# Two-block transformer kernel: order of the second attention, gate rows through memory, a stacked identity

## The chip, the cores and the metric

One NeuronCore of one Trainium2 chip runs the whole kernel. The metric is device microseconds of one execution; before the change the median of three runs is 2517.28 us (2514.53 to 2517.49).

## The reference, cut to what matters

Two transformer blocks on one sequence of 256 tokens, width 2048, all in float32. The first block has a gated convolution, a forgetting attention, a gate merge and a squared-ReLU feed-forward. The second block, which most of the change touches, is:

```python
mod = silu(c) @ w_ada + b_ada                      # six rows of 2048
shift_m, scale_m, gate_m, shift_f, scale_f, gate_f = split(mod, 6)
h = rms_norm(x, norm_mix_g) * (1 + scale_m) + shift_m
q, k, v, xs, z, bmat, cmat, dt_raw = split(h @ w_in, ...)
attn = rms_norm(attention(q, k, v, rel_bias), attn_norm_g)    # 8 heads of 128
ssm = ssd_mixer(xs, z, bmat, cmat, dt_raw, ...)    # y * silu(z), rms-normed in 2 groups
x = x + gate_m * (concat(attn, ssm) @ w_out)
h = rms_norm(x, norm_ffn_g) * (1 + scale_f) + shift_f
x = x + gate_f * conv_ffn(h, w_up, ..., w_down)
return rms_norm(x, final_norm_g)
```

## The kernel before, in words

**Weights.** Every weight matrix streams through the core once, in pieces of 1 MB. SyncE issues the load (`load`, L62) into one of three buffers `wraw`; ScalarE copies the piece to a rounded half `wH` (L126) and VectorE subtracts to get the rest `wL` (L127), three buffers each. TensorE multiplies both halves with activations that are split in the same way (chunks `act`, four buffers of four 128-channel tiles). `bblock` gives output channels by partition (two halves of 64 matmuls, each in a PSUM tile from a pool of two, evicted by L188 on ScalarE and L190 on VectorE); `ablock` gives tokens by partition (24 matmuls a piece). Nearly all matmuls have the line of the helper `mm`, L133.

**Order.** The body writes straight-line code; a planner orders each engine's instructions by program order as priority and by a simulated time, so that ready work of later stages fills gaps, and it hands out the buffers of a tag as they come free. `tc.high_priority()` lifts what is in it. Each engine then runs its list in order.

**Small sums.** `small_proj` multiplies by a matrix of n = 8 or 16 columns: high and low rows are stacked on 2n partitions, and four matmuls per token tile, with two slices of the identity, add and transpose them (tiles `wft`, `wdtt`; L133). Each such matmul shows as two instructions on TensorE.

**First norm.** After the first projection (`wide`, tiles `cc`) the sum of squares of x is reduced on TensorE (`rs0p`), raised to -1/2 on GpSimd (L290) and spread over the partitions (`bcast_tok`, `rbc0p`). VectorE scales `ccs` by it (L491, L502, L503) beside the projection `cb`.

**Second attention.** The projections q and k of both head groups come first (j = 0: q, k; j = 1: q, k), each with a piece of the state-space mixer in its middle (`ssm_prep`, `ssm_decay`, `ssm_out`). Then for each j: v (`ablock`), four heads (`heads`: scores `s`, softmax, transposes `pt`, product `o`) beside the projection z, then `cat` times silu(z) (L903, L905). `rms_ch` sums squares over `cat` for a norm: `ratt` for the eight heads, `rss0` and `rss1` for the two mixer groups. `cat_split` scales the four chunks of `cat` (L873) and splits them (L317, L318) into `act` buffers, which the four chunks of `h3` hold until the last projection of h3 has read them. The output projection `wo` (`ablock`, four pieces a column block) reads the four chunks in turn.

**Gates.** `mod` holds the six rows with channel as partition. `bcast_cols` turns gate_m (columns 32 to 47, `gm_bc`) and gate_f (80 to 95, `gf2`) into rows on all partitions by 16 transposes each (L306) and 4 copies on ScalarE (L307). `gm_bc` is used after each `wo` block, `gf2` in the down projection. Both lie in the tag `r8` (two buffers), where `gf2` follows the bias tile `toep`.

**End.** The last output block is cut into two halves of 256 columns in one PSUM bank (`dnl`).

Of the kernel before, what the change touches and what calls it, by code (L numbers as in the profile page):

```python
# [7 lines left out]
F32 = mybir.dt.float32  # L8
# [26 lines left out]
@with_exitstack  # L35
def body(ctx: ExitStack, tc: tile.TileContext, x_d, xT_d, vec_d, con_d, rel_d, relc_d, gfin_d, c_d, fg_d,
         wf_d, wdt_d, win_d, wv_d, wco_d, wao_d, wmix_d, wff1_d, wff2_d, wada_d, win2_d, wv2_d, wout_d, wup_d,
         wdn_d, rscr, xscr, out):
    nc = tc.nc
    V, A, T, G = nc.vector, nc.scalar, nc.tensor, nc.gpsimd  # L40

# [7 lines left out]
    def bank(name):  # L49
        return smp.tile([P, 512], F32, tag="sm", name=name)  # L50
# [39 lines left out]
    V.memset(mhalf, -0.5)  # L90
    warm = cp.tile([P, 2], F32, name="warm")
    A.activation(warm, mhalf, AF.Square)

    n_ada = [0]
    n_pc = [0]
# [171 lines left out]
    def small_proj(w_d, n, acts, name):  # L267
        raw = tp.tile([P, KT, n], F32, tag="t1k", bufs=6, name=name + "r")
        load(raw, w_d)
        hl = tp.tile([P, KT, 2, n], FR, tag="t2k", bufs=4, name=name + "hl")  # L270
        split(hl[:, :, 0, :], hl[:, :, 1, :], raw)
        ps = bank(name + "c")
        for k in range(KT):
            mm(ps[0:2 * n, :], hl[:, k].rearrange("p a n -> p (a n)"), acts[k][2], k == 0, k == KT - 1)
        c = tp.tile([P, 2, S], F32, tag="t2k", bufs=4, name=name + "s")
        A.activation(c[0:2 * n].rearrange("p a s -> p (a s)"), ps[0:2 * n, :], AF.Copy)
        tr = bank(name + "t")
        for t in range(2):
            ts = slice(t * P, (t + 1) * P)
            o = tr[:, t * n:(t + 1) * n]  # L280
            mm(o, c[0:2 * n, 1, ts], ident[0:2 * n, n:2 * n], t == 0, False)
            mm(o, c[0:2 * n, 1, ts], ident[0:2 * n, 0:n], False, False)
            mm(o, c[0:2 * n, 0, ts], ident[0:2 * n, n:2 * n], False, False)
            mm(o, c[0:2 * n, 0, ts], ident[0:2 * n, 0:n], False, True)
        return tr

    def pow_rstd(dst, ms_src, inv_n):
# [9 lines left out]
        A.activation(bc, ps[:, :S], AF.Copy)  # L297
        return bc

    def bcast_cols(cols, name):  # L300
        o = r8(name)
        for b in range(4):
            ps = bank(f"{name}p{b}")
            for k in range(4):
                i = 4 * b + k
                T.transpose(ps[:, k * P:(k + 1) * P], cols[:, i:i + 1].to_broadcast([P, P]), ident)  # L306
            A.activation(o[:, b * 512:(b + 1) * 512], ps, AF.Copy)  # L307
        return o

    def two(bc):  # L310
# [163 lines left out]
    with tc.high_priority():  # L474
        sacc = junk().rearrange("p (a s) -> p a s", a=2)
        for i in range(8):
            if i == 0:
                behind(A.activation(sacc, xT[:, 0:2, :], AF.Square), h1_last[0])
            else:
                sq = tp.tile([P, 2, S], F32, tag="t2k", bufs=4, name="sq0")  # L480
                behind(A.activation(sq, xT[:, 2 * i:2 * i + 2, :], AF.Square), h1_last[0])
                V.tensor_tensor(sacc, sacc, sq, op=OP.add)
    ps = bank("rs0p")
    for t in range(2):
        for b in range(2):
            mm(ps[:, t:t + 1], sacc[:, b, t * P:(t + 1) * P], ones[:, 0:1], t == 0 and b == 0, b == 1)
    rs0 = cp.tile([P, 2], F32, name="rs0")
    pow_rstd(rs0, ps[:, 0:2], 1.0 / D)
    rbc = bcast_tok(rs0, "rbc0")
    rbc2 = tp.tile([P, S], F32, tag="rbc2", bufs=1, name="rbc2")  # L490
    V.tensor_tensor(rbc2, rbc, rbc, op=OP.mult)  # L491

    cyh, cyl = cyc[:, :, 0, :], cyc[:, :, 1, :]
    for j in range(2):
# [202 lines left out]
    for c in range(N_FF // 2):  # L697
        if c == N_FF // 2 - 1:
            while n_ada[0] < 96:
                ada()  # L700
            V.tensor_tensor(mod, mod, vec[:, VEC["b_ada"]:VEC["b_ada"] + 96], op=OP.add)
            am = cp.tile([P, 16], F32, name="am")
            V.scalar_tensor_tensor(am, mod[:, 16:32], 1.0, vec[:, VEC["norm_mix_g"]:VEC["norm_mix_g"] + 16],
                                   op0=OP.add, op1=OP.mult)
            af = cp.tile([P, 16], F32, name="af")
            V.scalar_tensor_tensor(af, mod[:, 64:80], 1.0, vec[:, VEC["norm_ffn_g"]:VEC["norm_ffn_g"] + 16],
                                   op0=OP.add, op1=OP.mult)
            fls = rel_tiles()
            toep = r8("toep", (P, 8, S))
            for b in range(2):  # L710
                for k in range(2):
                    tps = bank(f"tps{b}{k}")
                    mm(tps, flip, fls[b][:, 2 * k:2 * k + 2, :].rearrange("p h c -> p (h c)"), True, True)
                    A.activation(toep[:, 4 * b + 2 * k:4 * b + 2 * k + 2, :].rearrange("p h c -> p (h c)"),  # L714
                                 tps, AF.Copy)
        u = us.pop(2 * c) + us.pop(2 * c + 1)
        ff2(c, u, 4 if c < N_FF // 2 - 1 else 3)
        for j in (2 * c + 3, 2 * c + 4):
            if j < N_FF:
                us[j] = ff1(j)  # L720
# [160 lines left out]
    ssm_x(1)  # L881


    qk = []
    for j in range(2):
        for hq, (nb, nm, sc) in enumerate(((0 + j, f"q2{j}", SCALE), (2 + j, f"k2{j}", None))):
            la = ssm_prep(j, hq)
            ms = []
            qk.append(bblock(win2_d, nb, h3, nm, q4([P, 4, S], nm + "T"), scale=sc,
                             mid=lambda: ms.extend(ssm_decay(j, hq, *la))))  # L890
            ssm_out(j, hq, ms, last_mm[0])
    gm_bc = None
    rss = []
    for j in range(2):
        ps = ablock(wv2_d, j, range(4), h3, f"v2{j}")
        vt = q4([P, 2, 512], f"vt2{j}")
        for t in range(2):
            A.activation(vt[:, t, :], ps[t], AF.Copy)
        heads(j, qk[2 * j], qk[2 * j + 1], vt, toep, lambda h, o: V.tensor_copy(cat[:, h, :], o))
        if j:  # L900
            ratt = rms_ch(0, 8, 1.0 / 1024, "ratt")
        z = bblock(win2_d, 6 + j, h3, f"z{j}", q4([P, 4, S], f"zs{j}"),
                   lambda hf, o: A.activation(o, o, AF.Silu))  # L903
        sl = slice(8 + 4 * j, 12 + 4 * j)
        V.tensor_tensor(cat[:, sl, :], cat[:, sl, :], z, op=OP.mult)  # L905
        if j == 0:
            rss.append(rms_ch(8, 4, 1.0 / 512, "rss0"))
            gm_bc = bcast_cols(mod[:, 32:48], "gm_bc")
    gf2 = bcast_cols(mod[:, 80:96], "gf2")
    ca = []  # L910
    cat_split(0, ratt, "attn_norm_g", 0, ca)
    cat_split(1, ratt, "attn_norm_g", 0, ca)
# [65 lines left out]
    def down_last(c, u):  # L978
        ws = [piece(wdn_d[n, c], 4, extra=None if n < 3 else True) for n in range(4)]
        rs4 = cp.tile([P, 2], F32, name="rs4")  # L980
        ss4 = cp.tile([P, 2, 5], F32, name="ss4")
        V.memset(ss4, 0.0)
        for t in range(2):
            ts = slice(t * P, (t + 1) * P)
            for n in range(4):
                h, l = ws[n]
                ps = bank(f"dnl{t}{n}")
                cuts = ((0, 512),) if t == 0 or n < 3 else ((0, 256), (256, 512))
                for j, (a, b) in enumerate(cuts):
                    for k in range(4):  # L990
                        mm(ps[:, a:b], u[k][0][:, ts], h[:, k, a:b], k == 0 and j == 0, False)
                        mm(ps[:, a:b], u[k][1][:, ts], h[:, k, a:b], False, False)
                    for k in range(4):
                        mm(ps[:, a:b], u[k][0][:, ts], l[:, k, a:b], False, k == 3)
                    cs = slice(n * 512 + a, n * 512 + b)
                    tm = tp.tile([P, 512], F32, tag="t2k", bufs=4, name="tm")
                    V.tensor_tensor(tm[:, a:b], ps[:, a:b], gf2[:, cs], op=OP.mult)
                    V.tensor_tensor(x3[:, t, cs], x3[:, t, cs], tm[:, a:b], op=OP.add)
                    A.activation(junk()[:, a:b], x3[:, t, cs], AF.Square, accum_out=ss4[:, t, n + j:n + j + 1])
                    if t and n == 3:  # L1000
                        y3 = tp.tile([P, 512], F32, tag="t2k", bufs=4, name="y3") if j == 0 else y3
                        V.tensor_tensor(y3[:, a:b], x3[:, t, cs], fg[:, cs], op=OP.mult)
                    else:
                        V.tensor_tensor(x3[:, t, cs], x3[:, t, cs], fg[:, cs], op=OP.mult)
            r = rs4[:, t:t + 1]
            V.tensor_reduce(r, ss4[:, t, :], axis=AX.X, op=OP.add)
            pow_rstd(r, r, 1.0 / D)
            for n in range(4):
                cs = slice(n * 512, (n + 1) * 512)
                src = y3 if t and n == 3 else x3[:, t, cs]  # L1010
                if n in (1, 3):
                    V.tensor_scalar(x3[:, t, cs], src, r, None, op0=OP.mult)
                else:
                    A.activation(x3[:, t, cs], src, AF.Copy, scale=r)
                if n % 2:
                    cs = slice((n - 1) * 512, (n + 1) * 512)
                    nc.sync.dma_start(out[0, ts, cs], x3[:, t, cs])
# [116 lines left out]
```

## Time and profile before

| | |
|---|---|
| Median of the runs shown | 2517.28 us |
| Profiled execution, whole | 2516.47 us |
| Its span in the trace | 2514.7 us |
| TensorE busy | 2479.3 us (99%) |
| VectorE busy | 1820.2 us (72%) |
| ScalarE busy | 1205.2 us (48%) |
| Mean granted TensorE clock | 0.994 |
| DMA | 571.66 MB, mean 227 GB/s |

The times of single instructions are those of the profiled execution; 1.8 us lie between its span and its whole time. A stage that ends later moves all behind it. TensorE is the engine whose idle time counts here; an idle VectorE or ScalarE counts only where TensorE waits for it.

### The profile page before, as it was taken

The page shows a single profiled execution, that of the slowest core. Times are in us where ns is not written, and L with a number is a line of the kernel's source. Part 1 is how long each engine was busy: PE and PEld are TensorE (multiplying, and loading weights), DVE is VectorE, ACT ScalarE, POOL GpSimd, SP SyncE. Part 2 cuts the span into 40 slices and gives each one's busy share as a digit, 9 for nine tenths or more (in the row PEclk, how much of TensorE's full clock was granted, in tenths as well). Part 3 has the DMA queues.
Part 4 walks back from the last instruction along what each step waited for, and adds up shares of the span by engine and source line. Part 5 has one row for each costly group of instructions (what it writes and reads, how often), then busy time and mean ns, then how long its engine had stood idle before and what let it go on. Part 6 is the DMA issues. An engine that isn't in the chain of part 4 may idle for free.

```text
span 2514.7 us, 31860 instructions
## 1 busy us (share of the span) xinstructions
PE 2479.3 (99%) x13178; PEld 2137.4 (85%) x13178; DVE 1820.2 (72%) x1995; ACT 1205.2 (48%) x1295; POOL 11.8 (0%) x16
## 2 busy tenths in 40 slices
PE   8999999999999999999999999989999999999998
PEld 7888888888888888888887888878888888888887
DVE  6777777787777777777657675565777777777777
ACT  6444444554544344444436544564644444444454
POOL 0000000000000000000000000000000000000000
PEclk9999999999999999999999999999999999999999
DMA  7677776678777777777755544445455555555553
GB/s 283 225 262 275 276 282 240 247 275 324 274 285 273 290 283 276 279 291 283 257 204 175 183 158 175 172 152 197 155 186 203 198 200 185 187 194 189 187 198 118
DMA packets 84258, 571.66 MB, mean 227 GB/s; under 512 B 9161, under 2 KB 10513, under 8 KB 16401
## 3 DMA queue, kind: packets, MB, share of 16 engines
q1 hardware_dynamic: 79488, 561.73, 61.1%
q10 hardware_dynamic: 4624, 7.89, 0.9%
q8 instruction: 103, 1.69, 0.3%
q14 instruction: 43, 0.34, 0.0%
HBM read 565.38 MB, written 4.21 MB: 227 GB/s over the span
## 4 chain that ended last, share of the span: by engine, by line
PE 98%; DVE 1%; issue 0%; ACT 0%; DMA 0%; POOL 0%; ACTq 0%; POOLq 0%
PE ff L133 28%; PE up L133 19%; PE dn L133 9%; PE k L133 4%; PE q L133 4%; PE gc L133 4%; PE ga L133 4%; PE v L133 3%; PE wo L133 3%; PE mix L133 3%; PE cc L133 3%; PE z L133 2%; PE co L133 2%; PE ao L133 2%; PE cb L133 2%; PE xsc0p L133 1%
## 5 line engine op out<-in xcount | busy, mean ns | idle before, releaser
L127 DVE TENSOR_TENSOR wL<-wraw,wH 128x2048 fp32r<-128x2048 f32 (+1 forms) x509 | 993.5, 1962 | 447.1 <-ACT wH L126 439.0
L126 ACT ACTIVATE wH<-wraw 128x2048 fp32r<-128x2048 f32 (+1 forms) x509 | 833.5, 1651 | 799.8 <-PE ff L133 290.6
L133 PE MATMUL up<-h4A,wH 128*128 128x512 f32 x1408 | 335.0, 390 | 0.0
L133 PEld LDWEIGHTS up<-h4A,wH 128*128 128x128 f32 x1408 | 260.0, 188 | 51.1
L103 DVE SCALAR_TENSOR_TENSOR wada<-wada,c_bc 128x2048 f32<-128x2048 f32 x96 | 219.7, 2288 | 36.9 <-DMA wada<-in_wada 36.7
L133 PE MATMUL ff<-g_mlpA,wH 128*128 128x512 f32 x1024 | 243.5, 390 | 0.0
L133 PEld LDWEIGHTS ff<-g_mlpA,wH 128*128 128x128 f32 x1024 | 188.9, 188 | 37.6 <-issue 0.6
L133 PE MATMUL ff<-wH,uh 128*128 128x512 f32 x496 | 193.1, 390 | 0.0
L133 PE MATMUL ff<-wH,ul 128*128 128x512 f32 x496 | 193.0, 389 | 0.0
L133 PEld LDWEIGHTS up<-h4A,wL 128*128 128x128 f32 x1408 | 178.5, 192 | 6.2 <-ACT h4A L368 1.0
L133 PE MATMUL up<-h4A,wL 128*128 128x256 f32 x1408 | 181.3, 283 | 0.7 <-ACT h4A L368 0.7
L133 PE MATMUL dn<-wH,vhl 128*128 128x512 f32 x640 | 158.1, 389 | 0.0
L133 PEld LDWEIGHTS dn<-wH,vhl 128*128 128x128 f32 x640 | 120.1, 188 | 24.9
L133 PEld LDWEIGHTS ff<-g_mlpA,wL 128*128 128x128 f32 x1024 | 129.5, 191 | 3.9
L133 PE MATMUL ff<-g_mlpA,wL 128*128 128x256 f32 x1024 | 130.9, 283 | 0.0
L133 PE MATMUL ff<-wL,uh 128*128 128x512 f32 x496 | 127.7, 389 | 0.0
L133 PEld LDWEIGHTS ff<-wH,uh 128*128 128x128 f32 x496 | 93.1, 188 | 19.7 <-ACT toep L714 0.4
L133 PEld LDWEIGHTS ff<-wH,ul 128*128 128x128 f32 x496 | 93.1, 188 | 19.4
L133 PEld LDWEIGHTS ff<-wL,uh 128*128 128x128 f32 x496 | 93.1, 188 | 19.3
L133 PE MATMUL dn<-wL,vhl 128*128 128x512 f32 x320 | 85.5, 389 | 0.0
L133 PEld LDWEIGHTS dn<-wL,vhl 128*128 128x128 f32 x320 | 60.1, 188 | 12.5
L133 PE MATMUL mix<-wH,mgA 128*128 128x512 f32 x256 | 62.1, 391 | 0.0
(569 smaller groups left out, 3171.4 us busy)
## 6 DMA issues: line engine op xcount, KB each, us to landing
wraw<-in_wff SPq DMA_DIRECT2D x128, 1024.0 KB, 4.8
wraw<-in_win SPq DMA_DIRECT2D x106, 1024.0 KB, 4.8
wada<-in_wada SPq DMA_DIRECT2D x96, 1024.0 KB, 4.9
wraw<-in_wup SPq DMA_DIRECT2D x88, 1024.0 KB, 4.7
wraw<-in_wdn SPq DMA_DIRECT2D x44, 1024.0 KB, 4.7
wraw<-in_wv SPq DMA_DIRECT2D x16, 1024.0 KB, 4.7
wraw<-in_wmix SPq DMA_DIRECT2D x16, 1024.0 KB, 5.0
wraw<-in_wout SPq DMA_DIRECT2D x16, 1024.0 KB, 4.8
```

What stands on the lines that cost most here:

```text
L103: V.scalar_tensor_tensor(w, w, 1.0, c_bc, op0=OP.mult, op1=OP.mult, accum_out=mod[:, i:i + 1])
L126: A.activation(h[:, sl], raw[:, sl], AF.Copy)
L127: ins = V.tensor_tensor(l[:, sl], raw[:, sl], h[:, sl].bitcast(F32), op=OP.subtract)
L133: return T.matmul(o, l, r, start=first, stop=last, skip_group_check=True)
```

## The change

```diff
 # small_proj: one matrix with two stacked identities
+        sl = sel[0:2 * n, 0:n]
+        V.tensor_tensor(sl, ident[0:2 * n, 0:n], ident[0:2 * n, n:2 * n], op=OP.add)
...
-            mm(o, c[0:2 * n, 1, ts], ident[0:2 * n, n:2 * n], t == 0, False)
-            mm(o, c[0:2 * n, 1, ts], ident[0:2 * n, 0:n], False, False)
-            mm(o, c[0:2 * n, 0, ts], ident[0:2 * n, n:2 * n], False, False)
-            mm(o, c[0:2 * n, 0, ts], ident[0:2 * n, 0:n], False, True)
+            mm(o, c[0:2 * n, 1, ts], sl, t == 0, False)
+            mm(o, c[0:2 * n, 0, ts], sl, False, True)
 # gates: 16 transposes and 4 copies each give way to a read of one row
-    def bcast_cols(cols, name):
+    def bcast_cols(row, name):
         o = r8(name)
-        for b in range(4):
...
+        A.dma_start(o, row.partition_broadcast(P))
 # ahead of rel_tiles(), in the last pass of the first feed-forward; mscr is (2, 2048) in memory
+            for i, c0 in enumerate((32, 80)):
+                A.dma_start(mscr[i].rearrange("(k p) -> p k", p=P), mod[:, c0:c0 + 16])
 # rs0p ... rbc0 ... rbc2: unchanged, now inside
+    with tc.high_priority():
 # second attention
+    q20 = proj2(0, 0)
+    k20 = proj2(0, 1)
+    q21 = proj2(1, 0)
+    attend2(0, q20, k20)
+    attend2(1, q21, proj2(1, 1))
+    ratt = rms_ch(0, 8, 1.0 / 1024, "ratt")
+    gm_bc = bcast_cols(mscr[0], "gm_bc")
     rss = []
     for j in range(2):
-        (v, heads; after the heads of j = 1: ratt)
         z = bblock(win2_d, 6 + j, h3, f"z{j}", ...)
         V.tensor_tensor(cat[:, sl, :], cat[:, sl, :], z, op=OP.mult)
         if j == 0:
             rss.append(rms_ch(8, 4, 1.0 / 512, "rss0"))
-            gm_bc = bcast_cols(mod[:, 32:48], "gm_bc")
-    gf2 = bcast_cols(mod[:, 80:96], "gf2")
+    gf2 = bcast_cols(mscr[1], "gf2")
 # last output block: the second half has a bank of its own
+                    if j:
+                        ps = bank("dnl_end")
-                        mm(ps[:, a:b], u[k][0][:, ts], h[:, k, a:b], k == 0 and j == 0, False)
+                        mm(ps[:, a:b], u[k][0][:, ts], h[:, k, a:b], k == 0, False)
```

`proj2(j, hq)` is the projection q or k of group j with its piece of the mixer as before; `attend2(j, q, k)` is v and the four heads. So the projections now run q0, k0, q1, v0, k1, v1, z0, z1, where they ran q0, k0, q1, k1, v0, z0, v1, z1.

## Rows read from the trace of the kernel before

**Rows 1.** Page, part 4: the chain that ended last, by engine.
```profile
PE 98%; DVE 1%; issue 0%; ACT 0%; DMA 0%; POOL 0%; ACTq 0%; POOLq 0%
```

**Rows 2.** Waits of TensorE: who, for whom, us in total, times, longest.
```profile
PE rattp L133 <- DVE ratta L861: 3.9, 1, 3.9
PE cc L133 <- DVE cbs L190: 2.1, 1, 2.1
PE dnl L133 <- DVE tm L997: 2.0, 1, 2.0
```

**Rows 3.** Chain in order of time, z to wo: start us, us, what.
```profile
1659.73 3.29 PE z L133 x20
...
1670.71 1.00 PE rattp L133 x4
...
1672.84 0.69 PE rattbp L295 x2
1673.53 3.41 PE gf2p L306 x16
1676.94 0.64 PE rss1p L133 x4
...
1683.85 81.40 PE wo L133 x359
```

**Rows 4.** Busy us (count) of each engine by window, then granted clock, DMA share, GB/s.
```profile
1663.00:1668.00 5.00, 1.90 (x11) 1.36 (x10) 3.92 (x6) 4.93 (x6) 0.00 (x0) 0.92 0.40 167
...
1673.00:1678.00 5.00, 5.00 (x24) 4.71 (x24) 4.02 (x10) 3.96 (x9) 0.00 (x0) 0.56 0.00 0
```

**Rows 5.** Timeline before wo: start us, us, engine, line, operation, count, idle before.
```profile
1673.98 3.26 DVE L873 SCALAR_TENSOR_TENSOR cat<-cat,vec,rattb 128x256 f32<-128x256 f32 x8 [1.75 <-ACT rattb L297]
...
1676.91 1.68 ACT L317 ACTIVATE catA<-cat 128x512 fp32r<-128x512 f32 x3
1677.15 1.29 DVE L318 TENSOR_TENSOR catA<-cat,catA 128x512 fp32r<-128x512 f32 x2
...
1677.44 4.15 PE L133 MATMUL wo<-wH,catA 128*128 128x512 f32 x16
```

**Rows 6.** Chain in order of time: gm_bc's transposes.
```profile
1631.42 1.31 PE gm_bcp L306 x12
```

**Rows 7.** Chain in order of time: the small sums.
```profile
161.40 1.88 PE wft L133 x16
...
1418.75 1.88 PE wdtt L133 x16
```

**Rows 8.** Timeline: first norm's steps, and matmuls behind two dips of the clock.
```profile
68.50 0.15 DVE L288 TENSOR_SCALAR rs<-rs0p 128x2 f32<-128x2 f32 x1
...
75.92 0.42 DVE L491 TENSOR_TENSOR rbc<-rbc 128x256 f32<-128x256 f32 x1
...
79.62 5.49 PE L133 MATMUL cc<-h1A,wH 128*128 128x512 f32 x16 [2.13 <-DVE cbs L190]
...
87.81 3.82 PE L133 MATMUL cc<-h1A,wH 128*128 128x512 f32 x16
...
1421.14 7.22 PE L133 MATMUL xsc0p<-h3A,wH 128*128 128x512 f32 x24
```

**Rows 9.** Windows with the granted clock at these two dips.
```profile
81.00:83.00 2.00, 2.00 (x6) 1.52 (x6) 2.00 (x3) 0.63 (x2) 0.00 (x0) 0.50 0.00 0
...
1422.00:1424.00 2.00, 2.00 (x6) 1.52 (x6) 1.33 (x4) 1.89 (x3) 0.00 (x0) 0.50 0.87 336
```

**Rows 10.** DMA queues: packets, MB, share of 16 engines' span.
```profile
q1 hardware_dynamic: 79488, 561.73, 61.1%
q10 hardware_dynamic: 4624, 7.89, 0.9%
```

**Rows 11.** Window of the first feed-forward's last passes.
```profile
1260.00:1280.00 20.00, 20.00 (x90) 16.57 (x89) 12.17 (x10) 7.36 (x4) 0.00 (x0) 1.00 0.58 211
```

**Rows 12.** Timeline at the end: VectorE takes the last 256 columns.
```profile
2506.47 0.42 DVE L997 TENSOR_TENSOR tm<-dnl,gf 128x256 f32<-128x256 f32 x1 [0.25 <-PE dnl L133]
```

More of the change, by code (lines that the diff above doesn't have):

```diff
@@ L37, in body @@
          wf_d, wdt_d, win_d, wv_d, wco_d, wao_d, wmix_d, wff1_d, wff2_d, wada_d, win2_d, wv2_d, wout_d, wup_d,
-         wdn_d, rscr, xscr, out):
+         wdn_d, rscr, xscr, mscr, out):
     nc = tc.nc
@@ L92, in body @@
     A.activation(warm, mhalf, AF.Square)
+    sel = cp.tile([P, 32], F32, name="sel")
     n_ada = [0]
@@ L298, in bcast_tok @@
         return bc
-    def bcast_cols(cols, name):
+    def bcast_cols(row, name):
         o = r8(name)
-        for b in range(4):
[L303 to L307, printed above, removed]
+        A.dma_start(o, row.partition_broadcast(P))
         return o
@@ L482, in body @@
                 V.tensor_tensor(sacc, sacc, sq, op=OP.add)
[L483 to L491, printed above, removed]
+    with tc.high_priority():
+        ps = bank("rs0p")
+        for t in range(2):
+            for b in range(2):
+                mm(ps[:, t:t + 1], sacc[:, b, t * P:(t + 1) * P], ones[:, 0:1], t == 0 and b == 0, b == 1)
+        rs0 = cp.tile([P, 2], F32, name="rs0")
+        pow_rstd(rs0, ps[:, 0:2], 1.0 / D)
+        rbc = bcast_tok(rs0, "rbc0")
+        rbc2 = tp.tile([P, S], F32, tag="rbc2", bufs=1, name="rbc2")
+        V.tensor_tensor(rbc2, rbc, rbc, op=OP.mult)
     cyh, cyl = cyc[:, :, 0, :], cyc[:, :, 1, :]
@@ L881, in body, with proj2, attend2 @@
     ssm_x(1)
[L884 to L894, printed above, removed]
+    def proj2(j, hq):
+        la = ssm_prep(j, hq)
+        ms = []
+        nm = f"{'qk'[hq]}2{j}"
+        o = bblock(win2_d, 2 * hq + j, h3, nm, q4([P, 4, S], nm + "T"), scale=None if hq else SCALE,
+                   mid=lambda: ms.extend(ssm_decay(j, hq, *la)))
+        ssm_out(j, hq, ms, last_mm[0])
+        return o
+    def attend2(j, qT, kT):
         ps = ablock(wv2_d, j, range(4), h3, f"v2{j}")
@@ L898, in body @@
             A.activation(vt[:, t, :], ps[t], AF.Copy)
-        heads(j, qk[2 * j], qk[2 * j + 1], vt, toep, lambda h, o: V.tensor_copy(cat[:, h, :], o))
-        if j:
-            ratt = rms_ch(0, 8, 1.0 / 1024, "ratt")
+        heads(j, qT, kT, vt, toep, lambda h, o: V.tensor_copy(cat[:, h, :], o))
+    q20 = proj2(0, 0)
[5 more added lines that the diff above has]
+    gm_bc = bcast_cols(mscr[0], "gm_bc")
+    rss = []
+    for j in range(2):
         z = bblock(win2_d, 6 + j, h3, f"z{j}", q4([P, 4, S], f"zs{j}"),
@@ L1128 @@
     args.append(nc.dram_tensor("x_scratch", (S, D), F32, kind="Internal").ap())
+    args.append(nc.dram_tensor("m_scratch", (2, D), F32, kind="Internal").ap())
     args.append(nc.dram_tensor("out_0_dram", (1, S, D), F32, kind="ExternalOutput").ap())
```

## The prediction

> **What bounds the kernel now.** I read the page first, then what TensorE waited for, then the chain of waits in order of time around the edits, and last the windows and the timeline there. The chain that ended last is TensorE's for 98% of the span [rows 1], so an edit is worth what it takes from TensorE's list, or from a hole in it. The list of TensorE's own waits is short, and three of them lie where this change works: before `rattp`, before a `cc` matmul, and in the last block [rows 2].
>
> The largest hole is at the end of the second attention. The last z matmul ends at 1659.73 + 3.29 = 1663.02 and the first `wo` matmul starts at 1677.44 [rows 3, 5]. In these 14.4 us the chain runs through the last heads, their norm `ratt`, its spreading, and `gf2`'s 16 transposes, because nothing of z is left to multiply and `wo` needs the normed chunks. The granted clock is at half in part of it: 0.92 in the first window (which takes in the last heads), 0.56 in the last [rows 4]. In the terms of the profile that is the lower level, 1.2 instead of 2.4 GHz.
>
> **The change part by part.** All terms are us against the profiled execution, 2516.47 (a span of 2514.7 and 1.77 around it); the median of the runs is 0.8 above it.
>
> *1. The hole before wo.* After the change both z projections stand behind the second group's heads. Each z takes some 22 us: 64 wide matmuls at `wo`'s pace, 64 x 81.40 / 359 = 14.5 [rows 3], and 64 half as wide, 7.3. So some 44 us of z lie behind v1 where 22 did. In the trace the second group's heads outlast their one z by the way to `rattp`, 1670.71 - 1663.02 = 7.7 [rows 3]. With a second z of 22 beside them `ratt` should be there over 10 us before z ends, and chunks 0 and 1 of `cat` can be scaled early. What stays at the seam is that their split goes into the buffers of `h3`, which z reads to its end: chunks 0 and 1 are let go one piece earlier, 5.5 us (24 `wo` matmuls at 81.40 / 359 [rows 3]). For chunk 0 the split costs two copies of 1.68 / 3 = 0.56 and two subtractions of 0.65 [rows 5], which fit there. The other group's norm, `rss1`, still follows z: but it is for chunk 3, and three pieces, 16.3 us of `wo`, stand before that. From the hole I keep as work 1.90 (the last heads, window 1663 to 1668 [rows 4]) and the three small steps 1.00 + 0.69 + 0.64 [rows 3], at full clock about half, 1.2: 14.4 - 1.9 - 1.2 = **11.3** saved, with `gf2`'s 3.41 in it. The 16 `wo` matmuls behind it took 4.15, against 3.82 for 16 at full clock [rows 5, 8]: **0.3**. What could be late next is the seam itself; it costs between 0 and 6.6 (second rival), and I take **-1.0**.
>
> *2. gm_bc.* Twelve of its 16 transposes took 1.31 on the chain, with TensorE full on both sides [rows 6]; 16 make **1.75**. The 8 copies on ScalarE hid beside matmuls.
>
> *3. The reads of the two rows.* Each puts 1 MB more on the queues, as a weight piece does. `gm_bc` is first needed behind the first `wo` block, four pieces or 22 us after `wo` begins, and `gf2` in the down projection, behind all 81.40 of `wo` [rows 3]: 0 by cover; without it one piece late, 5.5. Queued behind the issuing instruction on ScalarE are the `wH` copies; `gf2` waits for `toep`, which the last scores release before z, and `gm_bc`'s buffer was free long before. 0.
>
> *4. The writes of the two rows.* In the diff each partition's 16 values land 512 bytes apart, so nothing joins: 2 x 2048 elements of 4 bytes, 256 on each of 16 engines. The trace has no such transfer. From below 0. From above by the weight queue's packets: 0.611 x 16 x 2514.7 us / 79488 = 0.309 each, so 79 us of every engine. The nearest row is the other queue's 4624 packets of 1.7 KB on average: 0.009 x 16 x 2514.7 / 4624 = 0.078, so 20 us [rows 10]. I take that. The engines are 0.58 busy in this stage [rows 11], so 20 us fit beside the weights, and no reader comes before `gm_bc`, hundreds of us later. Cost on the path 0; if weights were held up altogether for 20 us, the three buffers of `wraw`, three times 5.5, leave a stall of 4. Behind the issue on ScalarE stand `wH` copies and `rel_tiles`' two reads, with TensorE at 20.00 of 20 and ScalarE at 7.36 [rows 11].
>
> By the Trainium skill (DMA: Bandwidth & Descriptors, section Rules for kernel authors) a strided last dimension becomes one descriptor per element, and one should rearrange so that it is contiguous. That speaks against these writes; no run here shows it yet, and what it would do to the time is the last rival.
>
> *5. Small sums.* Half of 16 instructions twice, 1.88 each [rows 7]: **1.88**. The added sum of identity slices is one small VectorE instruction with no need before the copy of the projection; 0. Behind `wdtt` the granted clock is 0.50 for a stretch [rows 9], and 24 `xsc0p` matmuls took 7.22 where 24 at full clock take 1.5 x 3.82 = 5.73 [rows 8]. Nothing else thin stands ahead of it for so long, and half as many thin matmuls should avoid it: 0 to 1.5, I take **1.5**.
>
> *6. First norm.* TensorE waited 2.13 for VectorE to empty a PSUM tile, and the eviction stood behind `rs0`'s chain: `rs` at 68.50, its square at 75.92, then `ccs`, then the eviction [rows 2, 8]. The lift brings the reduction and the spreading forward; some 7 us lie between 68.50 and 75.92 while the step needs about 2. So **2.1** goes. The clock behind it was 0.50 [rows 9], and 16 matmuls took 5.49 instead of 3.82 [rows 8]: **1.7**. If the order of VectorE stays, both are 0.
>
> *7. Last block.* TensorE's wait of 2.0 [rows 2] goes with a bank of its own, but VectorE is the bound there: it idled only 0.25 for the last 256 columns [rows 12]. 0 to 2.0; I take **0.25**, VectorE being full before.
>
> Sum: 11.3 + 0.3 - 1.0 + 1.75 + 1.88 + 1.5 + 3.8 + 0.25 = 19.8. That gives 2496.7 for the profiled execution, and 2497 for the median.
>
> **The rivals.**
>
> *The first norm's lift does nothing* (the planner keeps VectorE's order): 3.8 less, 2501. For it: the eviction was already under the same lift and was late all the same. Against: what it stood behind moves itself.
>
> *The seam stays.* Chunk 0's split is planned behind z's eviction, or the `h3` buffers come free later than I think. Then TensorE waits for an eviction and split, about 5, and the first 16 matmuls run slow by 1.7 again: 6.6 with the 1.0 already taken as 5.6 net, 2502.6. For it: four buffers for two sets of four chunks. Against: the planner places work when it is ready.
>
> *The heads give it back.* k1 now carries the first heads and `ssm_prep`, and v1 waits behind; if VectorE gets behind there (four heads, eight `wL`, 16 steps of `ssm_prep`), `ssm_out` stalls TensorE by some 7 with the slow clock after it, perhaps twice: 2504 to 2511. Against: over the span VectorE is busy 72% and ScalarE 48% (page, part 1), so both have room.
>
> *The element writes hold up the weights* (slower than before). Place: the first feed-forward, behind `mod`. If every element holds its engine and weights don't alternate with it, the stall is 256 x t less the 16.3 of the three buffers. It passes the gain of 20 from t = 36 / 256 = 0.14 us on; at 0.309 it is 63 us, so 2517 + 43 = 2560. For it: nothing of this size is in the trace. Against: the queue with the smaller packets has 0.078 each, and engines at 0.58 leave room for both.
>
> **How the numbers follow.** My forecast 60%, within 2491 to 2500; the lift does nothing 12%; the seam stays 14%; the heads give it back 8%; the element writes 6%. The range 2490 to 2509 takes the first three and most of the fourth. About 0.2% (5 us) is what a measurement can tell from no change: faster than 2512 holds in the first four, less a share for stalls I don't see: 0.88; within it 0.06; slower 0.06.
>
> **What would show it.** In the profile after: z followed by `wo` with under 2 us between, at full clock; no rows of `gm_bcp` and `gf2p`; `wft` and `wdtt` with 8 instructions each and no dip behind the second; no wait of `cc` for an eviction; `dnl` without its wait but an end hardly earlier. Wrong would be: a wait before `wo` over 5 us, a wait of `yp` or `s` within k1, or waits for `wraw` behind the writes of the rows.

## The result, and the profile after

The changed kernel took **2504.43 us** (median of 4 runs, 2501.51 to 2505.18) against 2517.04 for the kernel before in the same comparison: ratio 0.9950 [0.9935, 0.9964], so 12.6 us less, of 19.8 forecast, and inside the forecast range. Repeated later beside other kernels it took 2504.53 (ratio 0.9948 [0.9936, 0.9961]). The profiled executions compared below have spans of 2514.7 and 2503.4 us, a difference of 11.3, at the same mean clock of 0.994.

First the waits of TensorE after (for whom, us in total, times, longest), for [rows 2]:

```profile
PE trh L359 <- DVE xc L349: 6.7, 4, 2.6
PE wo L135 <- DVE catA L315: 2.9, 2, 1.5
PE cc L135 <- DVE cbs L192: 2.1, 1, 2.1
```

The waits of `rattp` and `dnl` are gone. (The first line is not new: before, these transposes waited 4.5 for `xc` and 2.6 for `ra`, 7.1 in all.) The wait of `cc` is as long as before, and `wo` has one that it did not have. The place of the old hole, in the chain of waits after (start us, us, what), for [rows 3]:

```profile
1656.49 2.29 DVE wL L129
1658.86 2.57 DVE cat L873 x7
...
1662.02 0.60 DVE catA L315
1662.62 0.60 DVE zs L192
1663.23 2.26 DVE wL L129
1665.48 0.61 DVE catA L315
1666.14 13.46 PE wo L135 x58
```

and in the timeline after (idle before in brackets), for [rows 5]:

```profile
1651.96 0.70 POOL L292 TENSOR_TENSOR rattr<-rattr,mhalf 128x2 f32<-128x2 f32 x1 [279.67 <-DVE rattr L290]
...
1656.49 2.29 DVE L129 TENSOR_TENSOR wL<-wraw,wH 128x2048 fp32r<-128x2048 f32 x1 [4.01 <-ACT wH L128]
1656.75 0.38 PE L297 MATMUL rattbp<-con,rattr 128*128 128x128 f32 x2
...
1658.77 3.25 DVE L873 SCALAR_TENSOR_TENSOR cat<-cat,vec,rattb 128x256 f32<-128x256 f32 x8
...
1659.68 0.63 ACT L314 ACTIVATE catA<-cat 128x512 fp32r<-128x512 f32 x1 [2.13 <-DVE cat L873]
...
1660.70 0.48 PE L135 MATMUL wo<-wH,catA 128*128 128x512 f32 x1
...
1662.68 2.11 PE L135 MATMUL wo<-wH,catA 128*128 128x512 f32 x8 [1.50 <-DVE catA L315]
...
1666.14 1.89 PE L135 MATMUL wo<-wH,catA 128*128 128x512 f32 x7 [1.36 <-DVE catA L315]
```

The hole of 14.4 us is now two waits of 1.50 and 1.36. The chain shows who is late: VectorE, without a pause, takes a weight piece's `wL` (2.29), eight scalings of `cat`, a split, the eviction of z and another `wL` (2.26) before the second split. The norm's value was there at 1651.96 + 0.70 = 1652.66, 8 us before the first `wo` at 1660.70. But its spreading `rattbp` stands in TensorE's list behind 24 matmuls of z and came 4.1 us later, at 1656.75; just before that VectorE had been idle for 4.01, and by then it had begun a `wL`.

The first norm's steps after, for [rows 8]:

```profile
68.27 0.15 DVE L290 TENSOR_SCALAR rs<-rs0p 128x2 f32<-128x2 f32 x1
...
75.69 0.42 DVE L489 TENSOR_TENSOR rbc<-rbc 128x256 f32<-128x256 f32 x1
...
78.55 1.28 DVE L192 TENSOR_TENSOR cbs<-cb,lo 128x512 f32<-128x512 f32 x2
79.39 5.47 PE L135 MATMUL cc<-h1A,wH 128*128 128x512 f32 x16 [2.13 <-DVE cbs L192]
```

Every step stands where it stood, 0.2 us earlier, and the 16 slow matmuls still take 5.47. The small sums, in the chain after, for [rows 7], have half their instructions (8, where there were 16):

```profile
161.15 0.98 PE wft L135 x8
...
1416.48 0.99 PE wdtt L135 x8
```

One place got longer with no edit near it: the norm ahead of the up projection. Windows there (busy us and count of TensorE, weight load, VectorE, ScalarE and GpSimd, then granted clock, DMA share, GB/s), before and then after:

```profile
1773.00:1775.00 2.00, 1.33 (x12) 1.31 (x12) 2.00 (x7) 1.80 (x5) 0.00 (x0) 1.00 0.73 291
```

```profile
1760.00:1762.00 2.00, 1.43 (x7) 1.36 (x7) 2.00 (x6) 1.84 (x5) 0.00 (x0) 0.50 0.74 307
```

and the first matmuls behind that norm in the timeline, before and then after:

```profile
1773.69 1.22 PE L133 MATMUL up<-h4A,wL 128*128 128x256 f32 x8 [0.67 <-ACT h4A L368]
```

```profile
1760.64 2.07 PE L135 MATMUL up<-h4A,wL 128*128 128x256 f32 x8 [0.57 <-ACT h4A L365]
```

The same eight matmuls in the same order, behind about the same wait, at 1.2 instead of 2.4 GHz. The clock was at half there for 3.4 us before and for 10.2 us after.

Followed by checkpoints that both traces have, the 11.3 us of the profiled executions come from these places:

| Place | Forecast | Profiled |
|---|---|---|
| first norm (term 6) | -3.8 | -0.2 |
| small sums (5) | -1.9 | -1.8 |
| clock behind `wdtt` (5) | -1.5 | -1.5 |
| norm ahead of the second attention (none) | 0 | +0.4 |
| first `xsc1p` to the end of `wo` (1 and 2) | -12.35 | -9.97 |
| norm ahead of the up projection (none) | 0 | +2.25 |
| end (7) | -0.25 | -0.5 |

The fifth row is the time from the first matmul of `xsc1p` to the end of `wo`: 1432.11 to 1765.25 before, 1429.03 to 1752.20 after.

### The profile page after: what moved, and what is told of

The parts are those of the page before. It is cut to its first block, busy times and chain, and to the rows that moved or that the text cites. A ratio compares the mean times of both kernels' runs of the same rounds, so it can differ in the third digit from the quotient of the medians.

```text
span 2503.4 us, 31758 instructions
## 1 busy us (share of the span) xinstructions
PE 2473.4 (99%) x13130; PEld 2132.3 (85%) x13130; DVE 1819.9 (73%) x1997; ACT 1195.8 (48%) x1283; POOL 9.7 (0%) x16
## 3 DMA queue, kind: packets, MB, share of 16 engines
q10 hardware_dynamic: 9040, 10.01, 1.3%
## 4 chain that ended last, share of the span: by engine, by line
PE 98%; DVE 1%; ACT 0%; issue 0%; DMA 0%; POOL 0%; ACTq 0%; POOLq 0%
PE ff L135 28%; PE up L135 20%; PE dn L135 9%; PE k L135 4%; PE q L135 4%; PE gc L135 4%; PE ga L135 4%; PE v L135 4%; PE mix L135 3%; PE wo L135 3%; PE cc L135 3%; PE co L135 2%; PE ao L135 2%; PE z L135 2%; PE cb L135 2%; PE bcsp L135 1%
## 5 line engine op out<-in xcount | busy, mean ns | idle before, releaser
L135 PEld LDWEIGHTS dn<-wL,vhl 128*128 128x128 f32 x320 | 60.1, 188 | 12.4
L135 PE MATMUL wo<-wH,catA 128*128 128x512 f32 x256 | 62.2, 391 | 2.9 <-DVE catA L315 2.9
```

What stands on the lines that cost most here:

```text
L135: return T.matmul(o, l, r, start=first, stop=last, skip_group_check=True)
```

## The experiments

All changes below are made to the changed kernel.

**old_order: is it the order that closes the hole?**

```diff
-    q20 = proj2(0, 0)
-    k20 = proj2(0, 1)
-    q21 = proj2(1, 0)
-    attend2(0, q20, k20)
-    attend2(1, q21, proj2(1, 1))
-    ratt = rms_ch(0, 8, 1.0 / 1024, "ratt")
...
+    qk = [proj2(j, hq) for j in range(2) for hq in range(2)]
...
     for j in range(2):
+        attend2(j, qk[2 * j], qk[2 * j + 1])
+        if j:
+            ratt = rms_ch(0, 8, 1.0 / 1024, "ratt")
         z = bblock(win2_d, 6 + j, h3, f"z{j}", ...)
...
```

> The changed kernel (2504.4 us) with the projections and heads of the second attention in the order of before (q0, k0, q1, k1, v0, z0, v1, z1); the rows still come through memory. Theory (the order alone closes the hole ahead of wo): the hole of 14.4 us is back without gf2's 3.4, about 11 against the 2.9 of waiting that the changed kernel has there, so 8 us slower than the changed kernel, about 2512; the wait of rattp is back in the list of TensorE's waits. Rival (most of the hole was the 16 transposes of gf2 at half clock and what they pushed back): under 3 us slower, 2507 or less.

Measured: 2515.38 (10 runs, 2511.93 to 2517.18), ratio to before 0.9994 [0.9984, 1.0003], some 3 us above the value of the theory that the order does it and far from its rival's. The waits of TensorE and the chain at the hole in this kernel:

```profile
PE rattp L135 <- DVE ratta L861: 3.9, 1, 3.9
...
PE wo L135 <- DVE catA L315: 1.6, 1, 1.6
```

```profile
1664.40 1.00 PE rattp L135 x4
...
1667.67 3.25 DVE cat L873 x8
...
1671.65 3.78 PE wo L135 x8
```

The wait for `ratta` is back at its old 3.9, and the memory rows, the stacked identity and the bank of its own cannot be told from no change without the new order. From the first `xsc1p` to the end of `wo` this kernel takes 333.4 in its profile, where the kernel before takes 333.1 and the changed one 323.2. So the order closes the hole. Taking `gf2`'s 3.41 us of transposes out did not shorten it by as much: where they lay TensorE now stands still, 1.6 of it for `catA`. And the eight `wo` matmuls at 1671.65 take 3.78, twice what eight take at full clock: the stretch at half clock lasts 13.7 us in this profile, into `wo`, where it lasted 10.2 before and ended with the hole.

**transposes: what are the rows through memory worth?**

```diff
-    def bcast_cols(row, name):
+    def bcast_cols(cols, name):
...
-        A.dma_start(o, row.partition_broadcast(P))
+        for b in range(4):
+            ps = bank(f"{name}p{b}")
+            for k in range(4):
+                i = 4 * b + k
+                T.transpose(ps[...], cols[:, i:i + 1].to_broadcast([P, P]), ident)
+            A.activation(o[:, b * 512:(b + 1) * 512], ps, AF.Copy)
...
-                A.dma_start(mscr[i].rearrange("(k p) -> p k", p=P), mod[:, c0:c0 + 16])
```

> The changed kernel with both rows made by 16 transposes and 4 copies each as before; nothing is written to or read from memory for them; the new order stays. Theory (the rows through memory cost nothing and save only the transposes, now at full clock): 2 x 16 transposes at 0.109 us are 3.5 us on TensorE, about 2508. Rival (the writes and reads of the rows ate the missing 7 us of my forecast by contention): the same as the changed kernel or faster, 2504 to 2500.

Measured: 2506.58 (5 runs, 2504.45 to 2507.54), ratio 0.9961 [0.9948, 0.9974]: 2.1 above the changed kernel, between the two expectations, with intervals that overlap. In the profile the stretch from the first `xsc1p` to the end of `wo` is 324.0 against 323.2, and the wait of `wo` is gone: `gf2`'s transposes run at 1666.1 to 1670.5, in the place where the changed kernel waits for VectorE. What the profile shows is small: 0.8 for 32 transposes.

**four_sums: are the thin matmuls the cause of the half clock behind them?**

```diff
-            mm(o, c[0:2 * n, 1, ts], sl, t == 0, False)
-            mm(o, c[0:2 * n, 0, ts], sl, False, True)
+            mm(o, c[0:2 * n, 1, ts], ident[0:2 * n, n:2 * n], t == 0, False)
+            mm(o, c[0:2 * n, 1, ts], ident[0:2 * n, 0:n], False, False)
+            mm(o, c[0:2 * n, 0, ts], ident[0:2 * n, n:2 * n], False, False)
+            mm(o, c[0:2 * n, 0, ts], ident[0:2 * n, 0:n], False, True)
```

> The changed kernel with four identity matmuls per token tile in the small sums, as before. Theory: 0.94 us more at wft and at wdtt, and a stretch at half clock behind wdtt again, 1.3 us: about 3.1 us slower, 2507.5. Rival (the stretch at half clock was not due to the thin matmuls but to the moment at which they fell): 1.9 us slower, 2506.3, with full clock behind wdtt.

Measured: 2505.92 (4 runs, 2504.89 to 2507.15), ratio 0.9962 [0.9947, 0.9977], 1.5 above the changed kernel, with intervals that overlap. Its chain and the window behind the sums:

```profile
1416.96 1.88 PE wdtt L135 x16
1418.84 9.91 PE xsc0p L135 x52
```

```profile
1419.00:1421.00 2.00, 2.00 (x12) 1.69 (x12) 1.68 (x6) 1.50 (x3) 0.00 (x0) 1.00 0.46 111
```

All 16 thin instructions are back, and the clock behind them stays full, as the rival had it; so it does in order_alone below, which has the 16 too. So thin matmuls alone do not bring the dip, and halving them can't be called the reason for the 1.5 us gained there. What set the clock there in the profile of before stays open.

**writes_x8 and writes_x2: how many element writes go unnoticed?** The two writes are repeated into rows that nobody reads, eight times and twice.

```diff
             for i, c0 in enumerate((32, 80)):
-                A.dma_start(mscr[i].rearrange("(k p) -> p k", p=P), mod[:, c0:c0 + 16])
+                for r in range(8):
+                    A.dma_start(mscr[2 * r + i].rearrange("(k p) -> p k", p=P), mod[:, c0:c0 + 16])
...
```

> The changed kernel with the writes of the two rows done eight times, into eight pairs of rows in memory: 16 writes of 2048 elements each where there were two; only the first pair is read. Theory (the writes hide beside the weights, whose queue they alternate with, and ScalarE has time to issue them): under 1 us, 2504 to 2505, with no wait of TensorE in the first feed-forward. Rival (they hold the engines or ScalarE, and the three weight buffers cover the two of the change but not sixteen): 0.14 us or more an element would be 16 x 128 x 0.14 = 287 us of each engine, and ScalarE's issues, 3.6 us the longer of the two, would be 16 x 3.6 = 57 us: a stall of tens of us in the first feed-forward, 2520 or more.

> The changed kernel with the writes of the rows done twice: four writes of 2048 elements. With sixteen, ScalarE stood up to 47 us behind its own issues and TensorE waited 78 us for wH. Theory (the issues queue up: the first two take 4 us, each one behind them 5 to 7, as the row of sixteen shows, and TensorE lives off three prepared pieces, 16 us): four cost 4 + 2 x 6 = 16 us on ScalarE, just covered: 0 to 3 us slower. Rival (the cost goes with their number, 78 us over 14 more writes, 5.6 each): 11 us slower, 2515.

Measured: with 16 writes 2588.37 (4 runs, 2586.24 to 2589.41), ratio 1.0287 [1.0269, 1.0304]; with 4 writes 2517.54 (11 runs, 2515.10 to 2521.54), ratio 1.0007 [0.9998, 1.0016], 13 above the changed kernel and so its whole gain. In both the rival held. The wait of TensorE with 16 writes, and then the same wait with 4:

```profile
PE ff L135 <- ACT wH L128: 77.9, 5, 41.6
```

```profile
PE ff L135 <- ACT wH L128: 9.5, 2, 5.6
```

What happens is seen on ScalarE with 4 writes (timeline; ACTq is its issuing of DMAs):

```profile
1243.27 4.55 ACTq L708 DMA_DIRECT2D m_scratch<-mod  x2
...
1247.85 16.01 ACTq L708 DMA_DIRECT2D m_scratch<-mod  x2
1263.91 0.63 ACT L641 ACTIVATE us<-us 128x512 f32<-128x512 f32 x1 [18.25 <-issue]
...
1287.31 1.91 ACT L128 ACTIVATE wH<-wraw 128x2048 fp32r<-128x2048 f32 x1 [13.58 <-DMA wraw<-in_wff]
```

Two writes are issued in 4.55 us, the next two hold ScalarE for 16.01, and no `wH` is made. After that the weights themselves are late: `wH` waits 13.58 for `wraw`. Of TensorE's two waits here 5.6 follow the first and 3.9 the second, and behind each the granted clock is at half for 6.8 us. In the changed kernel the two writes alone took this to issue, and to land (tile `m_scratch`; the 5.4 is the read of `gm_bc`, the writes landed after 15.7 and 29.1):

```profile
L707 ACTq DMA_DIRECT2D m_scratch<-mod x2: 389/1977/3565, 1242.9 to 1243.8; - x2
...
DMA to landing us min/median/max: 5.4/15.7/29.1
```

The windows around them, for [rows 11], the first line before and the others after:

```profile
1250.00:1255.00 5.00, 5.00 (x32) 4.44 (x31) 2.55 (x2) 2.64 (x3) 0.00 (x0) 1.00 0.42 177
```

```profile
1250.00:1255.00 5.00, 5.00 (x32) 4.43 (x30) 2.89 (x2) 1.87 (x3) 0.00 (x0) 1.00 0.57 31
...
1260.00:1280.00 20.00, 20.00 (x90) 16.58 (x89) 11.70 (x9) 7.68 (x4) 0.00 (x0) 1.00 0.92 282
```

and ScalarE's next weight pieces in the changed kernel:

```profile
1269.75 1.92 ACT L128 ACTIVATE wH<-wraw 128x2048 fp32r<-128x2048 f32 x1 [1.94 <-DMA wraw<-in_wff]
```

TensorE is full in all these windows, so the writes cost nothing. But while they were under way the weights all but stopped, 31 GB/s where it was 177, and were made up for later, with a DMA share of 0.92 where it was 0.58; twice as many writes already cost all that the change brings.

**cb_first: why did the lift do nothing?** Written without `tc.high_priority()`, the changed kernel has the same list of instructions on each of the five engines. So the lift moved nothing. In it the eviction of `cb` (L192) stands behind the four scalings of `ccs`. It goes into a buffer of the tag `q4`, which is handed out behind that of `y`, whose first write waits for the scaled `ccs`. In the lists, either a tag of its own for `cbs` or writing the projection `cb` ahead of `ccs` puts the first half of the eviction directly behind `rs`. The second was run:

```diff
+        cbs = bblock(win_d, 0, h1, "cb0", q4([P, 4, S], "cbs0")) if j == 0 else None
         for b in range(2):
...
-        bblock(win_d, 0 + j, h1, f"cb{j}", q4([P, 4, S], f"cbs{j}"), cb_done)
+        if j:
+            bblock(win_d, 0 + j, h1, f"cb{j}", q4([P, 4, S], f"cbs{j}"), cb_done)
+        else:
+            for hf in range(2):
+                cb_done(hf, cbs[:, 2 * hf:2 * hf + 2, :])
```

> The changed kernel with the first cb projection written ahead of y's arithmetic in the program (its product with y follows behind), nothing else. Theory (the eviction of cb stood behind the first norm's chain on VectorE because its buffer, of the tag q4, is handed out after y's, whose first write waits for that chain; the lift could not change that): the eviction moves ahead, TensorE's wait of 2.1 us before cc and the stretch at half clock behind it (1.7) go, 3.8 us faster than the changed kernel, about 2500.6. Rival (VectorE is simply late there): the wait stays, 0.

Measured: 2499.98 (5 runs, 2498.67 to 2500.69), ratio 0.9938 [0.9926, 0.9951]. Its timeline at the first norm:

```profile
68.16 0.68 DVE L192 TENSOR_TENSOR cbs<-cb,lo 128x512 f32<-128x512 f32 x1
...
76.92 3.79 PE L135 MATMUL cc<-h1A,wH 128*128 128x512 f32 x16
```

The first half of the eviction stands 10.4 us earlier, there is no wait of `cc` for it, and the 16 matmuls take 3.79 instead of 5.47. The `cc` block ends 4.2 us earlier in the profile, where the forecast had put 3.8.

**seam_order: can the wait at the seam, where z ends and `wo` begins, be won back?** Chunk 0's split is ordered ahead of the scaling of chunks 1 and 2 on VectorE, and the last piece of z behind `ratt`'s spreading on TensorE.

```diff
+            if i in (1, 2):
+                behind(ins, split0[0])
...
+                                if after is not None and hf == 1 and last and k == 0 and n == 0 ...:
+                                    behind(last_mm[0], after)
```

> The changed kernel with two orders written by hand at the seam from z to wo: the scaling of chunks 1 and 2 behind chunk 0's split on VectorE, and ratt's two spreading transposes ahead of the last piece of z on TensorE. Theory (wo waited 2.9 us since the planner had VectorE scale both attention chunks before it split chunk 0, and had the spreading late in z): the wait falls under 1 us, 2 to 3 us faster than the changed kernel, about 2502. Rival (the act buffers that z holds set the seam): the wait stays between 2 and 4 us, 0.

Measured: 2501.28 (5 runs, 2500.65 to 2504.46), ratio 0.9947 [0.9935, 0.9960], not to be told from the changed kernel's 0.9950. In its profile the wait of 2.9 is 1.6, now for chunk 1:

```profile
PE wo L135 <- DVE catA L317: 1.6, 1, 1.6
```

From the first `xsc1p` to the end of `wo` it takes 321.8, 1.4 less. The earlier spreading by itself gave nothing: the scaling of `cat` begins 9.40 us after `rattp` where it began after 9.48, for VectorE stands in the same `wL`. So the wait was in part one of order on VectorE; the whole time cannot show 1.4.

**both_fixes and both_again: the two together**, the second time beside the changed kernel unedited (changed_again).

> The changed kernel with both edits of the runs cb_first and seam_order. If both theories hold, 5 to 6.5 us faster than the changed kernel, 2498 to 2499.5; if the second norm's stretch at half clock (10.2 us here, 3.4 in the kernel before) is an accident of the moment and no part of the change, it differs between these runs without any edit near it, and moves each of them by up to 2 us.

> The changed kernel once more, unedited, to stand beside the others of this call on one chip: 0.995 of the kernel before. Its two waits before wo (2.9 us together) and the one before cc (2.1) are to come back; the lengths of the stretches at half clock in the two norms are not, if they are an accident of the moment.

> The kernel of run both_fixes, unedited, beside the changed kernel on one chip. Theory: 4 us from cb's eviction and 1.4 from the seam, of which cb's was shown whole and the seam's half (a wait of 1.6 stays, now for chunk 1): 5 us faster than the changed kernel, ratio to the kernel before 0.993. Rival (the seam's order gives nothing on the whole, and only cb's counts): 4 us, 0.9935.

Measured: 2498.32 (5 runs, 2496.05 to 2500.19), ratio 0.9935 [0.9922, 0.9949]; then 2499.76 (5 runs, 2496.53 to 2500.52), ratio 0.9928 [0.9915, 0.9940], beside 2504.53 for the changed kernel. This version beats both kernels, by 17.2 and 4.8 us; most of the 4.8 is cb_first's.

**order_alone: the order with the old transposes and the four sums** (the diffs of transposes and four_sums together).

> The new order of the second attention and the bank at the end alone: rows by transposes, four matmuls per token tile in the small sums, nothing through memory. Theory (the order closes the hole by itself, and the rest is worth only what TensorE no longer does: 1.9 us of thin matmuls and 1.75 of gm_bc, gf2's 16 transposes now filling the wait ahead of wo): 3 to 4 us slower than the changed kernel, ratio 0.9962 to 0.9966. Rival (the memory rows are needed to close the hole): 6 us or more slower, 0.9975 or above.

Measured: 2505.92 (5 runs, 2505.11 to 2506.16), ratio 0.9954 [0.9941, 0.9966]: 1.4 above the changed kernel in the same comparison, where 3 to 4 were expected. From the first `xsc1p` to the end of `wo` it takes 324.0 against 323.1 in changed_again. Another part is chance: at the norm ahead of the second attention the half clock lasted 3.4 us in this profile and 10.2 in that of changed_again. So the order, with the bank at the end, gives 11 of the 12.4 us; the 1.4 left to the small edits is within the intervals.

## Why the prediction was right in direction and range, and its gain 7 us too large

Of the signs that I had named, two failed: the wait of `cc` stayed, and 2.9 us of waiting, not under 2, lie at the seam from z to `wo`. That the time fell in the range is due to the largest term, the hole.

**The hole before wo (term 1): right in its mechanism, its size too large.** old_order shows that the order closes it. The terms -11.3, -0.3 and +1.0 with `gm_bc`'s -1.75 made 12.35, and 9.97 came. 1.9 of the difference is the seam: I charged 1.0, and 2.9 us of waiting stand there. I had looked for its cause in the buffers of `h3`; the chain shows VectorE, which had the splits, z's eviction and two `wL` to do at once, and seam_order took 1.4 off. I had z's second 22 us finish after `ratt` by over 10: the sum `rattp` did start at 1649.29, 11.4 before the first `wo`, but its spreading came only 4 before. One more thing changed with the order: ScalarE has 15 `ACT_TABLE_LOAD` instructions of 1.28 where before and old_order have 19, since fewer of z's silus fall between the softmaxes of the heads. No run tells what that alone is worth.

**gm_bc (2) and gf2: counted on the chain, worth less.** The 1.75 were on the path before. With the new order the transposes of `gf2` would fill the wait at the seam, so that both rows through memory together are worth 0.8 to 0.9 in the profiles of transposes and order_alone.

**Reads (3) and writes (4): nothing, as forecast, but not for the reason that I gave.** I had the writes fit beside the weights. In the changed kernel the weights all but stopped for some 10 us (31 GB/s, then 57, where before had 177 and 210), and ScalarE's `wH` waited 1.94, 0.55 and 1.79 for `wraw`, which I had named as a sign of being wrong. TensorE did not wait, because the pieces at hand covered it: my fallback, not my main argument. Nor is the 0.078 an element's price: in the packet records of the traces the 4-byte packets of that queue took 0.015 us each on average with two writes, 0.049 with four and 0.053 with sixteen. With these the last rival's formula, less the 16.3 of the three buffers, gives 9 for four writes and 93 for sixteen; 13 and 84 were measured. So the rival was near in size, but its place was half right: the longer waits of TensorE (5.6 of 9.5 with four writes, 73 of 77.9 with sixteen) lie behind ScalarE's issuing, and only the rest behind late weights. By the Trainium skill (DMA: Bandwidth & Descriptors, section Rules for kernel authors) a strided last dimension becomes one descriptor per element; the trace agrees, since this queue has 9040 packets after and 4624 before, 4416 more for 4096 elements and two reads.

**Small sums (5): right; the clock behind them right by accident.** 1.8 of 1.88 came. The dip is gone, but it is gone with 16 instructions too, so "half as many thin matmuls should avoid it" is not borne out, and the 1.5 is luck.

**The first norm (6): this step failed.** Of the 8.5 us missing between 19.8 and the 11.3 of the spans, 3.6 are here. The sentence "what it stood behind moves itself" was wrong: the lift moves no instruction, and the eviction stays behind it because its buffer is handed out in program order. My first rival, "the lift does nothing", was right, and its 2501 is nearer the measured 2504.4 than my 2497. cb_first shows that the price could be had. Only the 2.1 of waiting is sure, though: in old_order's profile the clock stayed full behind the same wait of 2.13, without any edit there.

**The end (7): right.** The wait of 2.0 is gone, and the end came 0.5 earlier, because VectorE now takes its last columns without a pause (timeline after, for [rows 12]):

```profile
2495.31 0.42 DVE L1007 TENSOR_TENSOR tm<-dnl_end,gf 128x256 f32<-128x256 f32 x1
```

**What I did not see: +2.25 at the norm ahead of the up projection.** No edit is near it. In the thirteen profiles the stretch at half clock there lasted 3.4 us six times, 6.8 twice and 10.2 five times. One and the same kernel had 3.4 there in both_fixes and 6.8 in both_again, and 3.4 and 10.2 at the norm ahead of the second attention; but the changed kernel had 10.2 in both its profiles. So whether the shift in time by the change favours the long stretch, or chance, stays open. With 3.6, this 2.25, the 2.4 of terms 1 and 2, 0.4 at the other norm and 0.1 at the small sums, less 0.25 at the end, the 8.5 are placed.

## What to carry to other kernels

A hole at the end of a stage is closed by moving independent work behind the late chain; then look at once at the engine that must feed the next stage, which here became VectorE. Before counting on a lift in priority, find what the late instruction waits for: here a buffer handed out in program order was not moved by priority, but by program order or a tag of its own. A transfer of single elements that costs nothing may be the last that costs nothing; repeat it to see how near the edge it is.

## What the runs showed of the hardware that was not expected

Writes of 2048 single elements held the engine that issued them: in the changed kernel the two took 0.39 and 3.57 us to issue, with four writes the second pair took 16.01, and ScalarE did nothing else meanwhile. The landing took up to 29.1 us, and in that time the weight loads of the other queue came nearly to a stop, with two writes already.

Waiting did not by itself bring the clock down: at the seam TensorE waited 1.50 and 1.36 us and worked 0.79 of 2 us in one window, at a granted clock of 1.00:

```profile
1664.00:1666.00 2.00, 0.79 (x4) 0.32 (x2) 2.00 (x2) 1.51 (x3) 0.00 (x0) 1.00 0.01 4
```

Behind a wait of 2.13 at the first norm it was at half in both kernels, but not in old_order's profile, where the same wait and the same 16 matmuls stand:

```profile
78.98 3.91 PE L135 MATMUL cc<-h1A,wH 128*128 128x512 f32 x16 [2.13 <-DVE cbs L192]
```

And the length of a stretch at half clock differs between two profiles of one kernel (3.4 and 10.2 us at one place, 3.4 and 6.8 at another), worth some 2 us of the whole; a difference of that size at a place that no edit touches can't be assigned to a change from one profile of each kernel.
